# Down projection: sums of activations made with the convolution and kept in HBM, 26 groups by seven instead of 22

## The chip, the cores and the metric

The kernel runs on one core of one Trainium2 chip. A core has a matrix engine (TensorE, PE in the profile), VectorE (DVE), ScalarE (ACT), GpSimd (POOL) and SyncE (SP); each runs its own queue of instructions in order, and they wait for each other by semaphores. The metric is the device time of one execution in microseconds (us), as the median of the runs.

## The reference

One layer of a hybrid block on 256 tokens of width 2048, all in float32: three attentions, a gated merge, and a feed-forward part. Only the last part matters here:

```python
    h2 = rms_norm(x, g_ffn[l])
    u = causal_depthwise_conv(h2 @ w_up[l], conv_w[l], conv_b[l])   # width 3 along the tokens
    u_gate, u_val = jnp.split(u, 2, axis=-1)                        # 5632 columns each
    x = x + (jax.nn.silu(u_gate) * u_val) @ w_down[l]               # w_down: 5632 x 2048
```

## The kernel before

**Precision.** Every float32 operand is split into a hi and a lo part that PE can take: ACT casts (hi), DVE subtracts (lo = value − hi). A product is then three matmuls, hi·hi, lo·hi and hi·lo (`three`, L1308 to L1311); for the weights this splitting is `parts` (L1300 to L1306).

**Up projection** (`u` tiles, L1219 and L1221). For 11 blocks of four column tiles, first gate then value, 16 row tiles of `w_up` in pieces of two. After a block, `conv` (L1131) makes the convolution, and for the value half (`s == 1`) the product with the silu of the gate, `g`; it splits `g` into `aT`, the activations of the down projection with hi and lo beside each other. `later` and `tick` spread these steps over the pieces of the next block. Beside this run `weight_sums` (L1168), one group of the down projection's weights at a time: they load two row tiles of `w_down` into r0 and r1, add, and store the sums T0 and T1 to HBM (`made`).

**Down projection** (`d` tiles). The 44 row tiles of `w_down` are taken in 22 groups of two (`k0`, `k1`), and the 2048 columns in two halves (`nb` = 0 and 1; `n0` = 0 and 1024), so a group is a 2 × 2 by 2 × 2 product of blocks: two tiles of activations by two halves of the tokens, two weight tiles by two blocks of 512 columns. A group *by eight* (`eight`, letter e) makes the eight block products, 24 matmuls in two steps. A group *by seven* (`seven`, letter s) makes seven products of sums of blocks, 21 matmuls in four steps: it needs four sums of activations (FS1 to FS4, made in `forms`) and four of weights: T4|T2 (one tile of 1024 columns) and T1|T3 (another). `gather` puts the products together at the end of a half.

**Sums of activations.** `forms(p)` takes `aT` back together from hi and lo with five operations on DVE, then ACT casts and DVE subtracts the split sums into `sf` (three of them) and into a free place of `aT` (FS4).

**Sums of weights.** T4|T2 comes from HBM in all groups. T1|T3 comes from HBM in the groups of `ALL_FOUR` (twelve); the other ten load the whole of `k0` and make it with two additions (L1371, L1372).

**Order.** `PLANS` gives the order of e and s in each half. Each step has a `prep` (loads, casts, subtractions, additions) and a `use` (matmuls); `prep` runs two steps ahead of `use` in the program (`AHEAD`), and the order on ACT, DVE and SP is kept as written (`keep`). hi and lo tiles have four buffers each (`SBUFS`), so the cast of a step waits until PE has ended with the step four before. Raw weights come into four buffers `raw`, and from the eleventh load on every third into two buffers `more`. Small tiles tagged `junk` have two buffers.

## Time and profile before

| | |
|---|---|
| median of 3 runs | 1472.62 us (1472.32 to 1474.24) |
| span of the profiled execution, first to last instruction | 1469.9 us |
| median less this span | 2.7 us |
| busy: PE, PEld, DVE, ACT, POOL | 1462.8, 1233.4, 1205.1, 895.3, 68.8 us |
| up projection on PE, 2816 matmuls | 747 to 1241 us |
| down projection on PE, first and second half | 1241 to 1357, 1357 to 1466 us |
| DMA traffic | 388.81 MB, mean 265 GB/s |

How it is read: times in the trace run from the first instruction. PE's matmuls overlap, so a busy PE says that it never ran dry, not that it was at its peak; PEld is the loading of weights into PE. A row of the timeline gives start, duration, engine, line, operation and tiles; a bracket at its end the idle time before it and what ended it.

### The profile page before, as it was taken

What the parts mean: (1) busy time and instruction counts of PE and PEld (TensorE: products, weight loads), DVE (VectorE), ACT (ScalarE), POOL (GpSimd) and SP (SyncE); (2) the same over time, 40 slices, a digit from 0 to 9 for tenths busy, and PEclk for the clock granted to TensorE, in tenths of its full rate; (3) what the DMA queues carried; (4) which work ended last, traced back from release to release, by engine and by line L of the source; (5) the groups of instructions that cost most, each with busy time, mean ns of one, the idle gap of its engine ahead of it and who ended that gap; (6) DMA issues with size and microseconds to landing.
All of it is one profiled execution on the core that took longest, in us unless ns stands there. A gap on an engine that the chain in (4) does not pass through costs nothing.

```text
span 1469.9 us, 20741 instructions
## 1 busy us (share of the span) xinstructions
PE 1462.8 (100%) x7327; PEld 1233.4 (84%) x7327; DVE 1205.1 (82%) x1617; ACT 895.3 (61%) x1287; POOL 68.8 (5%) x139
## 2 busy tenths in 40 slices
PE   9999999999999999999999999999999999999998
PEld 7888888888878888888888888888888888888887
DVE  5798767766997799888877888788887886998998
ACT  6755454454664466545657667567676777665774
POOL 1000001021000000000000000000000010000000
PEclk9999999999999999999999999999999999999999
DMA  8697898787766576866776888889888895778995
GB/s 295 202 341 260 265 313 270 226 294 267 256 221 204 204 271 247 287 222 237 273 239 218 302 272 276 294 277 310 295 265 273 280 305 190 249 256 286 334 315 191
DMA packets 163463, 388.81 MB, mean 265 GB/s; under 512 B 14016, under 2 KB 22512, under 8 KB 163360
## 3 DMA queue, kind: packets, MB, share of 16 engines
q1 hardware_dynamic: 150960, 345.34, 70.6%
q0 software_dynamic: 11648, 41.10, 7.3%
q8 instruction: 57, 0.93, 0.3%
q10 hardware_dynamic: 752, 1.06, 0.2%
q14 instruction: 46, 0.38, 0.1%
HBM read 349.70 MB, written 37.75 MB: 264 GB/s over the span
## 4 chain that ended last, share of the span: by engine, by line
PE 94%; DVE 3%; DMA 2%; issue 1%; ACT 0%; SPq 0%; DVEq 0%; ACTq 0%
PE u L1219 21%; PE u L1221 10%; PE d L1310 5%; PE d L1309 5%; PE d L1311 5%; PE g_x L769 4%; PE g_x L770 4%; PE g_x L771 4%; PE s L186 2%; PE s L188 2%; PE f L187 2%; PE f L188 2%; PE f L186 2%; PE s L187 2%; PE b L186 2%; PE b L188 2%
## 5 line engine op out<-in xcount | busy, mean ns | idle before, releaser
L1219 PE MATMUL u<-hT,hi_u 128*128 128x512 f32 x1408 | 442.6, 396 | 0.0
L1221 PEld LDWEIGHTS u<-hT,lo_u 128*128 128x128 f32 x1408 | 264.4, 188 | 63.5 <-DVE lo_u L176 1.1
L1221 PE MATMUL u<-hT,lo_u 128*128 128x256 f32 x1408 | 277.0, 278 | 0.7 <-DVE lo_u L176 0.7
L176 DVE TENSOR_TENSOR lo_u<-raw_u,hi_u 128x1024 fp32r<-128x1024 f32 x176 | 213.2, 1220 | 59.8 <-ACT hi_u L175 59.0
L175 ACT CAST hi_u<-raw_u 128x1024 fp32r<-128x1024 f32 x176 | 183.0, 1049 | 107.0 <-PE u L1219 54.6
L1219 PEld LDWEIGHTS u<-hT,hi_u 128*128 128x128 f32 x1408 | 214.5, 189 | 0.1
L764 ACT CAST hi_g<-raw_g 128x1024 fp32r<-128x1024 f32 (+1 forms) x96 | 91.1, 964 | 53.5 <-PE g_x L770 33.4
L765 DVE TENSOR_TENSOR lo_g<-raw_g,hi_g 128x1024 fp32r<-128x1024 f32 (+1 forms) x96 | 105.0, 1116 | 20.9 <-ACT hi_g L764 20.8
L769 PE MATMUL g_x<-hi_g,xT 128*128 128x512 f32 x251 | 98.8, 394 | 0.0
L770 PE MATMUL g_x<-hi_g,xT 128*128 128x512 f32 x251 | 97.7, 389 | 0.0
L771 PE MATMUL g_x<-lo_g,xT 128*128 128x512 f32 x251 | 96.3, 390 | 0.0
L1148 DVE TENSOR_TENSOR y<-y,z 128x512 f32<-128x512 f32 x88 | 60.7, 691 | 24.4 <-ACT z L1147 20.5
L1147 ACT ACTIVATE z<-u,taps 128x256 f32<-128x256 f32 x176 | 74.7, 496 | 0.0
L1309 PE MATMUL d<-hi_d,aT 128*128 128x512 f32 x176 | 68.5, 389 | 0.0
L1310 PE MATMUL d<-hi_d,aT 128*128 128x512 f32 x176 | 68.5, 389 | 0.0
L1311 PE MATMUL d<-lo_d,aT 128*128 128x512 f32 x176 | 68.1, 389 | 0.0
L175 ACT CAST hi_f<-raw_f 128x1024 fp32r<-128x1024 f32 (+1 forms) x40 | 38.6, 968 | 46.6 <-PE f L187 41.9
L186 PE MATMUL s<-hi_s,xT 128*128 128x512 f32 (+1 forms) x160 | 61.9, 387 | 0.0
L175 ACT CAST hi_b<-raw_b 128x1024 fp32r<-128x1024 f32 x32 | 33.6, 1052 | 45.2 <-PE b L187 23.5
L175 ACT CAST hi_s<-raw_s 128x1024 fp32r<-128x1024 f32 (+1 forms) x40 | 38.3, 959 | 36.8 <-PE s L187 29.3
L186 PE MATMUL f<-hi_f,xT 128*128 128x512 f32 (+1 forms) x160 | 60.4, 377 | 0.0
L188 PE MATMUL s<-lo_s,xT 128*128 128x512 f32 (+1 forms) x160 | 59.1, 369 | 0.0
(498 smaller groups left out, 3265.0 us busy)
## 6 DMA issues: line engine op xcount, KB each, us to landing
raw_u<-in_w_up_dram SPq DMA_DIRECT2D x176, 512.0 KB, 5.4
raw_g<-in_w_in_dram SPq DMA_DIRECT2D x86, 512.0 KB, 5.4
T<-r POOLq DMA_DIRECT2D x64, 512.0 KB, 6.1
r<-in_w_down_dram SPq DMA_DIRECT2D x88, 256.0 KB, 5.2
raw_d<-in_w_down_dram SPq DMA_DIRECT2D x44, 512.0 KB, 5.4
raw_f<-in_w_in_dram SPq DMA_DIRECT2D x32, 512.0 KB, 5.5
raw_s<-in_w_in_dram SPq DMA_DIRECT2D x32, 512.0 KB, 5.4
raw_s<-in_w_down_dram SPq DMA_DIRECT2D x32, 512.0 KB, 5.3
```

What stands on the lines that cost most here:

```text
L175: pin(nc.scalar.copy(hi[:, :m], raw[:, :m]))
L176: pin(nc.vector.tensor_tensor(lo[:, :m], raw[:, :m], hi[:, :m].bitcast(F32), ALU.subtract))
L186: nc.tensor.matmul(o, lhsT=xh, rhs=wh, start=first, stop=False)
L188: nc.tensor.matmul(o, lhsT=xh, rhs=wl, start=False, stop=last)
L769: nc.tensor.matmul(o, lhsT=a[0], rhs=w[0], start=first, stop=False)
L770: nc.tensor.matmul(o, lhsT=a[1], rhs=w[0], start=False, stop=False)
L771: nc.tensor.matmul(o, lhsT=a[0], rhs=w[1], start=False, stop=last)
L1219: nc.tensor.matmul(ps, lhsT=hi[:, j, c], rhs=hT[:, k + j, :], start=first, stop=False)
L1221: nc.tensor.matmul(ps[:, :S], lhsT=lo[:, j, c], rhs=hT[:, k + j, :S], start=False, stop=last)
L1309: nc.tensor.matmul(o, lhsT=ah, rhs=w[0], start=first, stop=False)
L1310: nc.tensor.matmul(o, lhsT=al, rhs=w[0], start=False, stop=False)
L1311: nc.tensor.matmul(o, lhsT=ah, rhs=w[1], start=False, stop=last)
```

## The change

- `unsplit_forms` makes the sums of activations of 16 groups inside `conv`, from `g` before it is split: three operations on DVE into the tile `y`, then a POOL DMA of 256 KB to HBM (`rforms`).
- `forms` no longer computes. It loads one set by a POOL DMA into a `junk` tile, and three ticks later ACT casts and DVE subtracts as before. In the first half ten of these are asked for in steps 1 to 10, in the second half six, one behind each of the first six groups by seven.
- `PLANS` has ten and sixteen groups by seven (8 and 14 before). The first group by seven comes after three by eight instead of five.
- `OWN` (eleven groups) load the two weight tiles whole and make all four weight sums with four additions in place, in `p1`. The other fifteen load both T tiles from HBM; `weight_sums` makes four sums for each of these fifteen, and is started every 9 pieces instead of 7.
- Every second raw load goes to `more`, which has four buffers; the tiles `t13` and `fr` of the down projection's pool go.

```diff
--- before.py
+++ after.py
@@ -35,8 +35,8 @@
 SBUFS = 4
 BLOCKS = 14
 WINDOW = 2
-PLANS = ("eeeee" + "se" * 5 + "sse" + "s" + "eee", "e" + "sse" * 4 + "ssse" + "sssee")
-ALL_FOUR = {(0, 6), (0, 7)} | {(1, p) for p in range(14) if p not in (4, 6, 8, 11)}
+PLANS = ("eee" + "sse" * 5 + "e" + "eee", "e" + "sssse" * 3 + "ssss" + "ee")
+OWN = {(0, p) for p in (1, 2, 4, 5, 7, 8, 9)} | {(1, 1), (1, 5), (1, 9), (1, 13)}
 AHEAD = 2
 GATE_PLANS = (("e" * 8, "essessee", "essessee"), ("eeesssee", "essessee", "essessee"))
 GATE_SEVENS = 4
@@ -48,6 +48,7 @@
 OUT_PLANS = ("eeesssee", "eessseee")
 OUT_SEVENS = 3
 NSEVEN = tuple(plan.count("s") for plan in PLANS)
+NFORM = max(NSEVEN)
 
 
 @with_exitstack
@@ -1162,10 +1163,26 @@
                 yield
             nc.vector.tensor_tensor(a[:, :, S:], g, a[:, :, :S].bitcast(F32), ALU.subtract)
             ended.append(f)
+            if f // 2 < NFORM:
+                yield 1
+                unsplit_forms(f // 2, g, y)
+
+    FS3, FS1, FS2, FS4 = range(4)
+    rforms = {}
+
+    def unsplit_forms(p, g, y):
+        v = g.rearrange("p k (t q) -> p (k t) q", t=NT)
+        r = y.rearrange("p k (t q) -> p (k t) q", t=NT)
+        tt = nc.vector.tensor_tensor
+        tt(r[:, :2], v[:, 0:4:3], v[:, 1:2].to_broadcast([P, 2, P]), ALU.subtract)
+        nc.vector.scalar_tensor_tensor(r[:, FS2], r[:, FS1], -1.0, v[:, 0], ALU.mult, ALU.subtract)
+        tt(r[:, FS4], r[:, FS2], v[:, 2], ALU.add)
+        rforms[p] = dram.tile([P, 512], F32, name=f"rform{p}")
+        nc.gpsimd.dma_start(rforms[p], y.rearrange("p k s -> p (k s)"))
 
     ended = []
     made = {}
-    asked = [(0, p) for p in range(NSEVEN[0])] + [(1, p) for p in range(NSEVEN[1])]
+    asked = [(nb, p) for nb in range(2) for p in range(NSEVEN[nb]) if (nb, p) not in OWN]
 
     def weight_sums(nb, p):
         n0 = nb * PIECE
@@ -1179,16 +1196,13 @@
             yield 1
         yield 1
         add = lambda o, i: tc.keep_in_program_order(nc.vector.tensor_tensor(o, o, i, ALU.add))
-        four = (nb, p) in ALL_FOUR
         add(r[0][:, 0], r[0][:, 1])
-        if four:
-            add(r[0][:, 1], r[1][:, 1])
+        add(r[0][:, 1], r[1][:, 1])
         yield 1
         add(r[1][:, 1], r[0][:, 0])
         add(r[1][:, 0], r[1][:, 1])
-        made[nb, p] = [dram.tile([P, PIECE], F32, name=f"T{j}_{nb}_{p}") for j in range(1 + four)]
-        if four:
-            nc.gpsimd.dma_start(made[nb, p][1], r[0].rearrange("p b n -> p (b n)"))
+        made[nb, p] = [dram.tile([P, PIECE], F32, name=f"T{j}_{nb}_{p}") for j in range(2)]
+        nc.gpsimd.dma_start(made[nb, p][1], r[0].rearrange("p b n -> p (b n)"))
         yield 1
         nc.gpsimd.dma_start(made[nb, p][0], r[1].rearrange("p b n -> p (b n)"))
 
@@ -1220,7 +1234,7 @@
                         else:
                             nc.tensor.matmul(ps[:, :S], lhsT=lo[:, j, c], rhs=hT[:, k + j, :S], start=False, stop=last)
                 n_ticks[0] += 1
-                if asked and n_ticks[0] > 8 and n_ticks[0] % 7 == 2:
+                if asked and n_ticks[0] > 8 and n_ticks[0] % 9 == 2:
                     adding.append([weight_sums(*asked.pop(0)), 0])
                 add_on()
                 tick()
@@ -1244,7 +1258,6 @@
 
     keep = tc.keep_in_program_order
     ov = out[0].rearrange("(t p) d -> p t d", p=P)
-    FS3, FS1, FS2, FS4 = range(4)
     sf = xt_pool.tile([P, 10, 3, 2, P], F32R, tag="xt", name="sf")
 
     def pieces_at(p):
@@ -1256,40 +1269,27 @@
     def form_of(p, f):
         if f == FS4:
             return pieces_of(p)[:, 0, :, 1]
-        if p < 10:
-            return sf[:, p, f]
-        return pieces_at(31 - p).rearrange("p k (f l q) -> p (k f) l q", f=2, l=2)[:, f]
+        return sf[:, p % 10, f]
 
     def forms(p):
 
-        flat = aT[:, 2 * p : 2 * p + 3].rearrange("p k s -> p (k s)").bitcast(F32)
-        v = flat[:, :1024].rearrange("p (k l t q) -> p k l t q", k=2, l=2, t=NT)
-        d = sm.tile([P, 512], F32, tag="junk", bufs=2, name=f"fd_{p}").rearrange("p (f l q) -> p f l q", f=2, l=2)
-        r = down_pool().tile([P, 512], F32, tag="fr", bufs=1, name=f"fr_{p}").rearrange("p (f q) -> p f q", f=4)
-        g = rbc.rearrange("p (k q) -> p k q", k=2)
-        two = flat[:, : 2 * 640].rearrange("p (a b) -> p a b", b=640)[:, :, :512]
-        two = two.rearrange("p a (l t q) -> p a l t q", l=2, t=NT)[:, :, :, 0]
-        tt = nc.vector.tensor_tensor
-        keep(tt(d, two, v[:, 0, :, 1].unsqueeze(1).to_broadcast([P, 2, 2, P]), ALU.subtract))
-        keep(tt(g, v[:, :, 0, 0], v[:, :, 1, 0], ALU.add))
-        keep(tt(r[:, :2], d[:, :, 0], d[:, :, 1], ALU.add))
-        keep(nc.vector.scalar_tensor_tensor(r[:, FS2], r[:, FS1], -1.0, g[:, 0], ALU.mult, ALU.subtract))
-        keep(tt(r[:, FS4], r[:, FS2], g[:, 1], ALU.add))
-        yield
-        to = sf[:, p] if p < 10 else form_of(p, slice(0, 3))
-        last = form_of(p, FS4)
+        r = sm.tile([P, 512], F32, tag="junk", bufs=2, name=f"fr_{p}").rearrange("p (f q) -> p f q", f=4)
+        keep(nc.gpsimd.dma_start(r.rearrange("p f q -> p (f q)"), rforms[p]))
+        yield 3
+        to, last = form_of(p, slice(0, 3)), form_of(p, FS4)
         keep(nc.scalar.copy(to[:, :, 0], r[:, :3]))
         keep(nc.scalar.copy(last[:, 0], r[:, FS4]))
         yield
-        keep(tt(to[:, :, 1], r[:, :3], to[:, :, 0].bitcast(F32), ALU.subtract))
-        keep(tt(last[:, 1], r[:, FS4], last[:, 0].bitcast(F32), ALU.subtract))
+        keep(nc.vector.tensor_tensor(to[:, :, 1], r[:, :3], to[:, :, 0].bitcast(F32), ALU.subtract))
+        keep(nc.vector.tensor_tensor(last[:, 1], r[:, FS4], last[:, 0].bitcast(F32), ALU.subtract))
+        issued.add(f"forms{p}")
 
     turn = [0]
 
     def buffer(name):
         turn[0] += 1
-        if turn[0] > 10 and turn[0] % 3 == 0:
-            return down_pool().tile([P, PIECE], F32, tag="more", bufs=2, name=name)
+        if turn[0] > 10 and turn[0] % 2 == 0:
+            return down_pool().tile([P, PIECE], F32, tag="more", bufs=4, name=name)
         return wp.tile([P, PIECE], F32, tag="raw", name=name)
 
     def load(src, name):
@@ -1351,34 +1351,37 @@
         k0, k1 = 2 * p, 2 * p + 1
         name = f"{n0}_{p}"
         w, raw = {}, {}
-        four = (n0 // PIECE, p) in ALL_FOUR
+        own = (n0 // PIECE, p) in OWN
+        add = lambda o, i: keep(nc.vector.tensor_tensor(o, o, i, ALU.add))
 
         def p0():
-            n = 512 if four else PIECE
+            n = PIECE if own else 512
             raw[0] = load(dv[:, k0, n0 : n0 + n], f"s{n0}_{k0}")
             (w["00"],) = parts(raw[0][:, :512], f"s{n0}_{k0}")
 
         def p1():
             raw[1] = load(dv[:, k1, n0 : n0 + PIECE], f"s{n0}_{k1}")
             w["10"], w["11"] = parts(raw[1], f"s{n0}_{k1}")
+            if own:
+                add(raw[0][:, :512], raw[0][:, 512:])
+                add(raw[0][:, 512:], raw[1][:, 512:])
+                add(raw[1][:, 512:], raw[0][:, :512])
+                add(raw[1][:, :512], raw[1][:, 512:])
 
         def p2():
-            raw[2] = load(made[n0 // PIECE, p][0], f"t{name}")
-            raw[3] = down_pool().tile([P, PIECE], F32, tag="t13", bufs=2, name=f"t13_{name}")
-            if four:
-                keep(nc.sync.dma_start(raw[3], made[n0 // PIECE, p][1]))
-            else:
-                keep(nc.vector.tensor_tensor(raw[3][:, :512], raw[0][:, :512], raw[0][:, 512:], ALU.add))
-                keep(nc.vector.tensor_tensor(raw[3][:, 512:], raw[0][:, 512:], raw[1][:, 512:], ALU.add))
-            w["T4"], w["T2"] = parts(raw[2], f"t42_{name}")
+            if not own:
+                raw[1] = load(made[n0 // PIECE, p][0], f"t{name}")
+                raw[0] = load(made[n0 // PIECE, p][1], f"t13_{name}")
+            w["T4"], w["T2"] = parts(raw[1], f"t42_{name}")
 
         def p3():
-            w["T1"], w["T3"] = parts(raw[3], f"t13_{name}")
+            w["T1"], w["T3"] = parts(raw[0], f"t13_{name}")
 
         def u0():
             three(Y()[0], *a_of(k0, 0), w["00"], first, last)
 
         def u1():
+            assert f"forms{p}" in issued
             three(X()[0][0], *a_of(k1, 0), w["10"])
             three(X()[0][1], *f_of(p, FS4), w["11"])
 
@@ -1444,7 +1447,6 @@
                     keep(nc.vector.tensor_tensor(xr, xr, banks[nb][0][t][n][:, oc], ALU.add))
                     (nc.scalar if nb else nc.gpsimd).dma_start(ov[:, t, xc], xr)
 
-    formed = 0
     after_step = {}
 
     def at(n, do):
@@ -1458,9 +1460,13 @@
         n_done = 0
         if nb == 0:
             at(-1, lambda: start(0))
+            for p in range(10):
+                at(p + 1, lambda p=p: later(forms(p)))
         for i, c in enumerate(plan):
             if c == "s":
                 seven(s, n0, X, Y, s == 0, s == ns - 1)
+                if nb and s + 10 < NFORM:
+                    at(len(steps), lambda p=s + 10: later(forms(p)))
                 s += 1
                 if s == ns:
                     at(len(steps) - 1, lambda nb=nb: later(gather(nb, banks[nb][1])))
@@ -1469,10 +1475,7 @@
                 n_done += 1
                 if n_done == 4:
                     at(len(steps) - 1, lambda nb=nb: residual(nb))
-                if formed < ns and n_done >= 4 - 3 * nb:
-                    at(len(steps) - 2, lambda p=formed: later(forms(p)))
-                    formed += 1
-        assert s == ns and not straight and formed >= ns
+        assert s == ns and not straight
         at(len(steps) - 1, finish)
         at(len(steps) - 1, lambda nb=nb: results(nb))
         if nb == 0:
```

Three places in the order of instructions. First ScalarE in the first half, from the second group by seven (group 1) to the group by eight behind it. Names: `hi_t42_0_1` is the cast of T4|T2 of group 1, `hi_s0_3` is row tile 3 (k1 of group 1), `fr_4` the loaded sums of group 4, `hi_d0_26` row tile 26 of a group by eight. Before:

```order
L1304 CAST hi_s0_3_12155<-raw_s0_3_12153 128x1024
L1281 CAST sf_11814<-fr_2_12147 128x3x128
L1282 CAST aT_6836<-fr_2_12147 128x128
L1304 CAST hi_t42_0_1_12178<-raw_t0_1_12173 128x1024
L1304 CAST hi_t13_0_1_12187<-t13_0_1_12175 128x1024
L1304 CAST hi_d0_28_12199<-raw_d0_28_12197 128x1024
```

And now:

```order
L1304 CAST hi_s0_3_12047<-raw_s0_3_12045 128x1024
L1304 CAST hi_t42_0_1_12061<-raw_s0_3_12045 128x1024
L1280 CAST sf_11826<-fr_2_12008 128x3x128
L1281 CAST aT_6836<-fr_2_12008 128x128
L1280 CAST sf_11826<-fr_3_12010 128x3x128
L1281 CAST aT_6836<-fr_3_12010 128x128
L1304 CAST hi_t13_0_1_12072<-raw_s0_2_12026 128x1024
L1280 CAST sf_11826<-fr_4_12024 128x3x128
L1281 CAST aT_6836<-fr_4_12024 128x128
L1304 CAST hi_d0_26_12090<-raw_d0_26_12088 128x1024
```

Before, one set of sums, which DVE had made, was copied ahead of the casts of T4|T2 and T1|T3. Now sets 2 and 3 are copied between these two casts, and set 4 ahead of the cast for the next group by eight.

Second, VectorE at the same group. Before:

```order
L1305 TENSOR_TENSOR lo_s0_3_12156<-raw_s0_3_12153,hi_s0_3_12155 128x1024
L1371 TENSOR_TENSOR t13_0_1_12175<-raw_s0_2_12128 128x512
L1372 TENSOR_TENSOR t13_0_1_12175<-raw_s0_2_12128,raw_s0_3_12153 128x512
L1305 TENSOR_TENSOR lo_t42_0_1_12179<-raw_t0_1_12173,hi_t42_0_1_12178 128x1024
L1284 TENSOR_TENSOR sf_11814<-fr_2_12147,sf_11814 128x3x128
```

And now:

```order
L1305 TENSOR_TENSOR lo_s0_3_12048<-raw_s0_3_12045,hi_s0_3_12047 128x1024
L1355 TENSOR_TENSOR raw_s0_2_12026<-raw_s0_2_12026 128x512
L1355 TENSOR_TENSOR raw_s0_2_12026<-raw_s0_2_12026,raw_s0_3_12045 128x512
L1355 TENSOR_TENSOR raw_s0_3_12045<-raw_s0_3_12045,raw_s0_2_12026 128x512
L1355 TENSOR_TENSOR raw_s0_3_12045<-raw_s0_3_12045 128x512
L1305 TENSOR_TENSOR lo_t42_0_1_12062<-raw_s0_3_12045,hi_t42_0_1_12061 128x1024
L1305 TENSOR_TENSOR lo_t13_0_1_12073<-raw_s0_2_12026,hi_t13_0_1_12072 128x1024
L1283 TENSOR_TENSOR sf_11826<-fr_2_12008,sf_11826 128x3x128
```

Before, T4|T2 came from HBM as `raw_t0_1`; now it is the result of the four additions, in the buffers of the raw weights, and the tile that ACT casts is the one that DVE has just written.

Third, GpSimd's queue in the first half of the down projection as it is now (before, only the four `xr` loads stood there).

```order
L1277 DMA fr_0_11901<-rform0_7417 128x512
L1277 DMA fr_1_11929<-rform1_7422 128x512
L1404 DMA xr_0_0_0_12166<-xkeep0_6082 128x512
L1404 DMA xr_0_0_1_12168<-xkeep1_6083 128x512
L1404 DMA xr_0_1_0_12170<-xkeep0_6082 128x512
L1277 DMA fr_2_12008<-rform2_7878 128x512
L1404 DMA xr_0_1_1_12172<-xkeep1_6083 128x512
L1277 DMA fr_3_12010<-rform3_7883 128x512
L1277 DMA fr_4_12024<-rform4_8333 128x512
```

The loads of the sums stand in this queue, between those of the residual.

## Prediction

> **What bounds the kernel now.** I began with the page's busy shares by slice and its chain, then asked who waits for whom on TensorE (PE), then for tables by stage, and last for the timelines of one pair of steps in the down projection.
>
> ```profile
> PE   9999999999999999999999999999999999999998
> DVE  5798767766997799888877888788887886998998
> ...
> PE 94%; DVE 3%; DMA 2%; issue 1%; ACT 0%; SPq 0%; DVEq 0%; ACTq 0%
> ```
>
> ```profile
> PE u L1221 <- DVE lo_u L176: 0.7, 1, 0.7
> ...
> PE g_y L769 <- ACT hi_g_0t L764: 0.2, 1, 0.2
> ```
>
> ```profile
> 1270.00:1300.00 30.00, 30.00 (x134) 24.84 (x133) 29.70 (x46) 18.73 (x25) 0.00 (x0) 1.00 0.71 247
> 1300.00:1330.00 30.00, 30.00 (x134) 24.85 (x133) 29.36 (x40) 20.20 (x24) 0.00 (x0) 1.00 0.84 286
> ...
> 1355.00:1385.00 30.00, 30.00 (x134) 24.84 (x133) 27.78 (x40) 20.28 (x25) 3.24 (x6) 1.00 0.97 352
> ```
>
> PE never stops, and its waits (the second block: total, times, longest) come to about 1 us. So the time is the number of matmuls times their spacing. But in the down projection VectorE (DVE, the third busy time in a row of the table) is busy 29.70 of 30 us. It holds PE's pace with nothing to spare, and any chain that runs through it is at the edge.
>
> ```profile
> 1268.28 0.39 PE L1309 MATMUL d<-hi_s,aT 128*128 128x512 f32 x1
> ...
> 1273.04 0.39 PE L1309 MATMUL d<-hi_d,aT 128*128 128x512 f32 x1
> ...
> 1278.47 0.39 PE L1309 MATMUL d<-hi_s,aT 128*128 128x512 f32 x1
> ```
>
> A group by seven is 21 matmuls in 1273.04 − 1268.28 = 4.76 us, one by eight 24 in 5.43. One matmul costs 0.227 us; its 0.39 overlaps the next.
>
> ```profile
> 1280.72 2.35 DVE L1305 TENSOR_TENSOR lo_d<-raw_d,hi_d 128x1024 fp32r<-128x1024 f32 x2
> 1282.99 0.68 DVE L1305 TENSOR_TENSOR lo_s<-raw_s,hi_s 128x512 fp32r<-128x512 f32 x1
> 1283.59 0.68 DVE L1273 TENSOR_TENSOR fd<-aT 128x512 f32<-128x512 f32 x1
> ...
> 1285.52 1.22 DVE L1305 TENSOR_TENSOR lo_s<-raw_s,hi_s 128x1024 fp32r<-128x1024 f32 x1
> 1286.65 0.68 DVE L1371 TENSOR_TENSOR t<-raw_s 128x512 f32<-128x512 f32 x1
> ...
> 1287.86 1.22 DVE L1305 TENSOR_TENSOR lo_t<-raw_t,hi_t 128x1024 fp32r<-128x1024 f32 x1
> 1288.99 0.55 DVE L1284 TENSOR_TENSOR sf<-fr,sf 128x384 fp32r<-128x384 f32 x1
> ...
> 1289.77 1.23 DVE L1305 TENSOR_TENSOR lo_t<-t,hi_t 128x1024 fp32r<-128x1024 f32 x1
> 1290.92 2.35 DVE L1305 TENSOR_TENSOR lo_d<-raw_d,hi_d 128x1024 fp32r<-128x1024 f32 x2
> ```
>
> Start to start, DVE pays 1.13 us for a subtraction of 1024 columns, 0.60 for one of 512, 1.93 for the five operations that make sums of activations (1283.59 to 1285.52), 0.78 for splitting them (1288.99 to 1289.77). A whole seven and eight take it 10.20 us; PE takes 4.76 + 5.43 = 10.19.
>
> **The change, part by part.**
>
> *Matmuls.* 26 groups by seven for 22 save 4 × 3 × 0.227 = **2.7 us**. That is all the change can win on PE.
>
> *The up projection.* 18 of 78 weight additions go, 16 sets of three operations come.
>
> ```profile
> L176 DVE TENSOR_TENSOR lo_u<-raw_u,hi_u 128x1024 fp32r<-128x1024 f32 x176 | 213.2, 1220 | 59.8 <-ACT hi_u L175 59.0
> ```
>
> At the spacings above the additions are 18 × 0.6 = 11 us less, the new sets about 16 × 1 = 16 us more. DVE idles 59.8 us before this one line, which covers the 5 us. I take 0; without the cover an addition held up at the wrong place costs what the one wait above did, 0.7 us, so the ends are +2 (three such) and −0.7 (that wait gone).
>
> *Own weight sums.* In eleven sevens the cast of T4|T2 on ScalarE (ACT) must follow four additions, each on the one before. The spacing of such additions, and a hand-over from ACT to DVE:
>
> ```profile
> 1349.69 0.68 DVE L1417 TENSOR_TENSOR xr<-xr,e 128x512 f32<-128x512 f32 x1
> 1350.41 0.69 DVE L1418 TENSOR_TENSOR e<-e,d 128x512 f32<-128x512 f32 x1
> ```
>
> ```profile
> 1268.29 1.05 ACT L1304 CAST hi_t<-t 128x1024 fp32r<-128x1024 f32 x1 [1.67 <-PE d L1310]
> ...
> 1285.31 0.51 ACT L1281 CAST sf<-fr 128x384 fp32r<-128x384 f32 x1 [1.04 <-DVE fr L1276]
> 1285.72 0.29 ACT L1282 CAST aT<-fr 128x128 fp32r<-128x128 f32 x1
> 1285.97 1.06 ACT L1304 CAST hi_t<-raw_t 128x1024 fp32r<-128x1024 f32 x1
> ```
>
> ```profile
> 1269.37 1.23 DVE L1305 TENSOR_TENSOR lo_t<-t,hi_t 128x1024 fp32r<-128x1024 f32 x1 [0.82 <-ACT hi_t L1304]
> ```
>
> Additions: 3 × 0.72 + 0.69 = 2.85 us. Hand-over: 1269.37 − (1268.29 + 1.05) = 0.03 us. The first ACT row also shows the ring at work: a cast waits for PE to leave the buffer of four steps before.
>
> Take an own seven right behind another seven. Its k1 cast gets its buffer when PE ends the last product with the hi half of the previous k1. From there: cast 1.05, subtraction 1.13, additions 2.85, cast 1.05, four hand-overs 0.12: 6.20 us. PE reaches the first T4|T2 product 23 spacings after that last one began, 5.21 − 0.39 = 4.82 us after it ended. Wait: **1.4 us**. Five sevens stand so (group 7 of the first half; 1, 5, 9, 13 of the second): 7.0 us.
>
> Groups 5 and 9 of the first half follow another own one. From cast to cast DVE and ACT then do 1.13 + 1.13 + 0.60 + 1.13 + 2.85 + 1.05 + 0.1 = 8.0 us, PE 4.76; the wait is at most 3.2, less what the first had in hand. I take 2.8 each, 5.6 us (ends 1.4 and 3.2 each).
>
> Group 1 pays the 1.4 and more: the first seven comes four steps of an eight earlier (4 × 2.7 = 10.9 us), just as DVE ends the convolution's tail, so there is little lead, and its k1 load is one of a burst. I take 4.5 (ends 1.4 and 6). Groups 4 and 8 follow an eight and cost about nothing; group 2 also does, but starts without lead: 1.0.
>
> *Reloading the sums of activations.* Each set now comes by a POOL DMA into one of two buffers, so load p + 2 waits until DVE has subtracted set p. ACT copies a set in its own order, ahead of casts that PE needs next. The nearest load of this size and queue:
>
> ```profile
> xr<-xkeep POOLq DMA_DIRECT2D x8, 256.0 KB, 5.0
> ```
>
> ```profile
> DMA to landing us min/median/max: 3.7/5.0/7.3
> ```
>
> Set 4: after DVE's last subtraction for group 1 come sets 2 and 3, and load 4 can go 0.67 us later; 5.0 to land, 0.66 for two copies (spacings 0.41 and 0.25), 1.05 for the cast of the next eight, 0.1 for hand-overs: 7.5 us. PE has four matmuls left in that time, 0.9 us, so it waits 6.5, then 0.8 for the subtraction: **7.3 us**. Set 8 stands the same way before group 3, with a cast of 512 columns (0.62): 6.1, and then set 9's copies hold the next casts, about 1.5: 7.6. Sets 2, 3 and 6, 7 stand between the casts of T4|T2 and T1|T3 in groups 1 and 2: 1.3 + 1.05 against six matmuls, then the subtraction, 1.7 us each: 3.4. Sum 18.3. With loads of 3.7 it is 15.7, of 7.3 it is 22.9, for two round trips; the nearest row to all is the median, which I take. The page "DMA: Bandwidth & Descriptors" of the Trainium skill (section "Anatomy of one DMA — SWDGE (gpsimd) path") puts such a DMA at about 2.0 us plus its bytes over 436 GB/s, 2.6 us here (an estimate), which would make the time 4.8 us shorter. All eight loads in the row above took longer, so I don't use it.
>
> In the second half sets 10 to 15 are asked for a group or more ahead and stand behind casts that wait for PE anyway. The bytes there, per four sevens and an eight (24.5 us), are 3 × 1.84 MB (256 + 3 × 512 KB with sums from HBM) and 2 × 1.05 (2 × 512 KB): 311 GB/s, and the table above shows 352 carried without a wait. I cost both at nothing; if that cover goes, one late 512 KB load costs about 1.5 us, and I keep +3 for it.
>
> *Sum:* −2.7 + 7.0 + 5.6 + 4.5 + 1.0 + 18.3 = **+33.7**, and I add 1.5 for the second own group of the second half, whose set copies stand beside its additions, and for short waits: **+35 us**. On the execution's span of 1469.9 that is 1505; the median of the runs, 1472.6, has 2.7 us around the span, so I predict **1508 us**.
>
> A check without any DMA: in the first half's five pairs of sevens and an eight DVE needs 10 × 4.0 + 7 × (2.85 + 1.1 for the cast it waits for) + 5 × 2.27 + 10 × 0.78 = 87 us, PE 75. At most a ring of four steps, 4.8 us, is in hand. So 7 us are lost there even if every set is early, 5.6 in the second half by the chain: 1482 at the least by this.
>
> **Rivals.**
>
> 1. *Sets arrive in time* (ACT gets to the copies later than I think). Then only the own sums count: 35 − 18.3 = +17, 1489. For it: POOL has little else to do. Against: the buffer is free only 0.7 us before the copies stand next on ACT. 10%.
>
> 2. *The own sums hide* and only reloads cost: 35 − 18 = +17, 1490. For it, a row of the gate stage, where sums are made the same way:
>
> ```profile
> ACT hi_g_2t L764 <- DVE raw_g L810: 10.9, 4, 2.8
> ```
>
> ACT waited for these additions, PE only the 0.2 us above. Against: there T1|T3 goes first, which needs two additions, not four. 8%.
>
> 3. *All hides*, so no slower: 1469.9, a gain of 0.18%, within the 0.2% that a measurement can tell from none. The place is the ring of four buffers on DVE and ACT. It decides if a cast of T4|T2 comes within 4.82 us of its buffer's release, so if four additions took 1.4 us and not 2.85, and sets landed before they are asked for. DVE's 29.70 of 30 us is against it. 5%.
>
> 4. *The clock falls.*
>
> ```profile
> 1445.00:1470.00 25.00, 20.64 (x92) 16.75 (x90) 19.02 (x23) 9.32 (x10) 0.00 (x0) 0.97 0.40 150
> ```
>
> ```profile
> 1465.41 0.24 PE d L1311
> ```
>
> A mean of 0.97 over 25 us is 1.5 us at half clock, so it halved at about 1468.5, 2.9 us after the last product ended. The two waits of some 6 us are longer than that. How long half clock then lasts no row shows; between nothing and a whole seven (4.76 us) lost each, with loads at their slow end (+4.6): 1508 to 1522, say 1515. 17%. The page "TensorE: Matmul & The Clock Gate" of the Trainium skill (Part 1, "What's actually happening") says half clock comes after an idle window of about 3.4 us and goes after as much sustained work; by that each wait adds 1.7 us (an estimate), 3.4 in all.
>
> **How the numbers follow.** Forecast 60%, its own range 1499 to 1517 (the ends of group 1, the pairs and the loads). With rival 4's to 1526 and rivals 1 and 2 from 1488, a good 8 in 10 are held. Slower: 94%; within 0.2%: 4%; faster: 2% (rival 3 split).
>
> **What would show it.** Right: in the changed profile PE waits for ACT's hi_t by 1 to 3 us in eight or so places, and twice for some 6 us in the 60 us after the first group by seven, with ACT waiting for fr's DMA ahead of them; the second half some 6 to 8 us longer than its matmuls; 12 matmuls fewer; the up projection as long as before. Wrong: ACT's waits for fr short (the sets were early), or PE's waits for hi_t missing behind own sums.

## The result, and the profile after

| | before | after |
|---|---|---|
| median of the runs | 1472.82 us (1472.32 to 1474.24) | 1514.71 us (1512.32 to 1514.87) |
| span of the profiled execution | 1469.9 us | 1510.6 us |
| matmuls of the down projection | 990 | 978 |
| first to last product of the down projection (starts) | 224.2 us | 263.6 us |

The change makes the kernel slower by 2.84% (ratio 1.0284, 95% interval 1.0269 to 1.0299). One of the eleven runs of eights_first_8, below, took 1603.84 us at a granted clock of 0.851; it is counted in that row's median and not in its ratio. The up projection takes 493.3 us in both traces. Of 40.7 us more in the span, 39.4 lie between the first and the last product of the down projection; the other 1.2 are 1.5 us more behind the last product, less 0.2 ahead of the first.

The lines of the page that answer to those of before are TensorE's (PE's) and VectorE's (DVE's) busy tenths, the granted clock in tenths, and the chain that ended last:

```profile
PE   9999999999999999999999999999999996889998
...
DVE  5798676766997899978878888888878766787987
...
PEclk9999999999999999999999999999999998899999
...
PE 87%; DVE 4%; DMA 3%; issue 3%; ACT 3%; POOL 0%; SPq 0%; ACTq 0%; DVEq 0%; POOLq 0%
```

PE's row was nines up to the last digit; now three slices stand at 6 and 8, in the first half of the down projection. PE's share of the chain fell from 94% to 87%; ScalarE (ACT) went from 0% to 3%, issue from 1% to 3%, DMA from 2% to 3%. DVE, which was the engine at its edge, is less busy there than before, so it is not its amount of work that holds PE up. Two rows of the table by stage (PE, PEld, DVE, ACT, POOL; granted clock; DMA) say the same of the worst stretch; before, PE was busy for 30.00 of 30 us in both, and DVE for 29.70 and 29.36:

```profile
1270.00:1300.00 30.00, 18.24 (x57) 11.82 (x57) 15.70 (x24) 11.08 (x20) 3.22 (x6) 0.82 0.50 171
1300.00:1330.00 30.00, 25.85 (x103) 20.05 (x104) 25.36 (x30) 17.90 (x23) 0.00 (x0) 0.90 0.51 163
```

The waits of PE in the down projection (total, times, longest), where before there was none:

```profile
PE d L1309 <- ACT hi_t L1304: 15.3, 10, 2.7
PE d L1309 <- ACT hi_s L1304: 7.5, 2, 6.1
PE d L1309 <- ACT hi_d L1304: 5.7, 1, 5.7
PE d L1311 <- DVE lo_t L1305: 1.1, 2, 0.5
```

There are two main kinds. The ten waits for hi_t, the hi half of a tile of weight sums, are mostly behind own sums. One of them, group 1 of the second half (PE's rows first, then ACT's, then DVE's):

```profile
1400.65 0.61 PE L1311 MATMUL d<-lo_s,aT 128*128 128x512 f32 x2
1402.61 0.50 PE L1309 MATMUL d<-hi_t,sf 128*128 128x512 f32 x1 [1.34 <-ACT hi_t L1304]
...
1396.32 1.05 ACT L1304 CAST hi_s<-raw_s 128x1024 fp32r<-128x1024 f32 x1 [0.47 <-PE d L1310]
1401.51 2.00 ACT L1304 CAST hi_t<-raw_s 128x1024 fp32r<-128x1024 f32 x2 [4.14 <-DVE raw_s L1355]
...
1397.40 1.23 DVE L1305 TENSOR_TENSOR lo_s<-raw_s,hi_s 128x1024 fp32r<-128x1024 f32 x1 [0.21 <-ACT hi_s L1304]
1398.54 0.68 DVE L1355 TENSOR_TENSOR raw_s<-raw_s 128x512 f32<-128x512 f32 x1
1399.26 1.42 DVE L1355 TENSOR_TENSOR raw_s<-raw_s,raw_s 128x512 f32<-128x512 f32 x2
1400.71 0.69 DVE L1355 TENSOR_TENSOR raw_s<-raw_s 128x512 f32<-128x512 f32 x1
```

Cast (1396.32), subtraction (1397.40), four additions (1398.54 to 1401.40), cast (1401.51): one chain, in which ACT and DVE wait for each other in turn, and PE's bracket of 1.34 us is what it is too long by.

The second kind is the two waits of some 6 us. The first, for set 4 of the sums of activations:

```profile
1275.62 1.21 POOL L1277 DMA_DIRECT2D fr<-rform  x2 [11.38 <-DVE aT L1284]
...
1279.97 0.51 ACT L1280 CAST sf<-fr 128x384 fp32r<-128x384 f32 x1 [6.81 <-DMA fr<-rform]
1280.39 0.29 ACT L1281 CAST aT<-fr 128x128 fp32r<-128x128 f32 x1
1280.59 1.04 ACT L1304 CAST hi_d<-raw_d 128x1024 fp32r<-128x1024 f32 x1
...
1281.68 0.79 PE L1309 MATMUL d<-hi_d,aT 128*128 128x512 f32 x1 [5.65 <-ACT hi_d L1304]
```

POOL asks for the set when DVE has split the sets before it (11.38 us of waiting for DVE aT), the load lands 4.35 us later, and behind ACT's wait for it (6.81) stands the cast hi_d that PE needs.

A third kind is small. In group 0 PE loses 1.5 us, and in group 1 another 2.3 ahead of the products with own sums. There ACT waits for weights that are still on their way: T1|T3 of group 0, which comes from HBM, and the two row tiles of group 1.

```profile
1260.20 1.05 ACT L1304 CAST hi_t<-raw_t 128x1024 fp32r<-128x1024 f32 x1 [4.16 <-DMA raw_t<-T]
1262.43 0.62 ACT L1304 CAST hi_s<-raw_s 128x512 fp32r<-128x512 f32 x1 [1.18 <-DMA raw_s<-in_w_down_dram]
1264.76 1.04 ACT L1304 CAST hi_s<-raw_s 128x1024 fp32r<-128x1024 f32 x1 [1.70 <-DMA raw_s<-in_w_down_dram]
```

### The profile page after: what moved, and what is told of

Read it like the earlier page. It is cut to its first block, busy times and chain, and to the rows that moved or that the text cites. A ratio compares the mean times of both kernels' runs of the same rounds, so it can differ in the third digit from the quotient of the medians.

```text
span 1510.6 us, 20765 instructions
## 1 busy us (share of the span) xinstructions
PE 1472.1 (97%) x7315; PEld 1230.2 (81%) x7315; DVE 1206.8 (80%) x1613; ACT 898.0 (59%) x1299; POOL 84.0 (6%) x167
## 2 busy tenths in 40 slices
DMA packets 160840, 384.89 MB, mean 255 GB/s; under 512 B 13952, under 2 KB 22448, under 8 KB 160736
## 3 DMA queue, kind: packets, MB, share of 16 engines
q10 hardware_dynamic: 752, 1.06, 0.2%
## 4 chain that ended last, share of the span: by engine, by line
PE 87%; DVE 4%; DMA 3%; issue 3%; ACT 3%; POOL 0%; SPq 0%; ACTq 0%; DVEq 0%; POOLq 0%
PE u L1233 20%; PE u L1235 10%; PE g_x L770 4%; PE g_x L771 4%; PE g_x L772 4%; PE d L1309 3%; PE d L1310 3%; PE d L1311 3%; PE f L189 2%; PE f L188 2%; PE f L187 2%; PE s L187 2%; PE s L189 2%; PE s L188 2%; PE b L188 2%
## 5 line engine op out<-in xcount | busy, mean ns | idle before, releaser
L1309 PE MATMUL d<-hi_d,aT 128*128 128x512 f32 x144 | 57.1, 396 | 5.7 <-ACT hi_d L1304 5.7
L187 PE MATMUL f<-hi_f,xT 128*128 128x512 f32 (+1 forms) x160 | 60.4, 377 | 0.0
L189 PE MATMUL f<-lo_f,xT 128*128 128x512 f32 (+1 forms) x160 | 59.0, 369 | 0.0
L188 PE MATMUL f<-hi_f,xT 128*128 128x512 f32 (+1 forms) x160 | 59.0, 369 | 0.0
```

Of the source, the lines that this page charges most:

```text
L187: nc.tensor.matmul(o, lhsT=xh, rhs=wh, start=first, stop=False)
L188: nc.tensor.matmul(o, lhsT=xl, rhs=wh, start=False, stop=False)
L189: nc.tensor.matmul(o, lhsT=xh, rhs=wl, start=False, stop=last)
L1309: nc.tensor.matmul(o, lhsT=ah, rhs=w[0], start=first, stop=False)
```

## The experiments

Every run is compared with the kernel before, run beside it on the same chip (its medians were 1471.9 to 1472.7 us). Theory A holds that the loss has three causes: the chain of own sums, the reload of the sets, and TensorE's clock, which falls to half behind the long waits. In the changed kernel 23 matmuls ran at half clock; their spacings (0.43 us or more, less 0.227 each) add up to 1.54 + 1.67 + 2.24 = 5.45 us. So the clock seemed to be the missing part of the prediction.

| run | median us | ratio to before, 95% interval | first to last product, us |
|---|---|---|---|
| changed kernel | 1514.71 | 1.0284 (1.0269 to 1.0299) | 263.6 |
| spread_loads | 1497.84 | 1.0177 (1.0162 to 1.0193) | 248.0 |
| no_own_adds | 1497.10 | 1.0166 (1.0150 to 1.0183) | 245.4 |
| no_adds_spread | 1474.40 | 1.0016 (1.0007 to 1.0026) | 224.7 |
| t13_first | 1501.43 | 1.0197 (1.0182 to 1.0212) | 251.8 |
| behind_eights | 1504.65 | 1.0218 (1.0203 to 1.0234) | 256.2 |
| third_buffer | 1513.84 | 1.0281 (1.0266 to 1.0296) | 264.0 |
| fill_waits | 1516.67 | 1.0304 (1.0286 to 1.0321) | 267.7 |
| fill_again | 1517.47 | 1.0298 (1.0282 to 1.0315) | 268.2 |
| fill_all | 1515.19 | 1.0289 (1.0275 to 1.0303) | 265.4 |
| spread_fill | 1494.06 | 1.0149 (1.0132 to 1.0166) | 246.6 |
| eights_first | 1472.74 | 1.0005 (0.9995 to 1.0015) | 224.0 |
| eights_first_8 | 1470.65 | 0.9985 (0.9976 to 0.9994) | 221.8 |

The last column is of one profiled execution each. Each interval reaches 0.001 to 0.002 to either side, some 2 us, so a difference between two rows is known to about 3 us.

### Taking each cause away, and both

*spread_loads*: the sets of the first half are asked for at the pace at which they are used.

```diff
-            for p in range(10):
-                at(p + 1, lambda p=p: later(forms(p)))
...
+                if not nb:
+                    at(max(s + 1, len(steps) - 6), lambda p=s: later(forms(p)))
                 seven(s, n0, X, Y, s == 0, s == ns - 1)
```

> The changed kernel with one edit: the ten sets of the first half are asked for six steps before their group's first step (one set in some four steps) and no longer one in each step from the second on. Theory A (three causes: the chain of own sums, the reload through two buffers, the clock that falls behind its two long waits): the waits of TensorE for hi_d and hi_s of 5.7 and 6.1 us go, the granted clock stays at 1.0 in the whole down projection, and the waits for hi_t behind a seven stay (2.9, 2.5, 1.5, 2.9 us in the first half, 1.5 us four times in the second). By the gaps of the changed kernel that is 5.8 + 6.3 + about 1.5 behind them, and 5 to 6 us of half clock: 1514.7 - 19, 1492 to 1499. Theory B (the reload alone costs): 1472. Theory C (VectorE has too much to do with the own sums, or the DMA too much to bring, and the reload only shows where that comes up): 1508 to 1515, since the work is the same.

16.9 us under the changed kernel, within theory A's range; B and C fall. The two long waits are gone, and PE's largest now is of another kind:

```profile
PE d L1310 <- DVE aT L1284: 9.5, 4, 2.7
PE d L1309 <- ACT hi_t L1304: 5.4, 4, 1.4
```

In the first half the waits of own sums are seen one product earlier, since the pieces of a set (aT) now queue behind the additions on DVE. One part of the expectation missed: the clock did not stay at 1.0. It fell behind each of three waits of 2.9 us, and 5.9 us of slow spacing are left.

*no_own_adds*: the four additions are left out.

```diff
-            if own:
-                add(raw[0][:, :512], raw[0][:, 512:])
-                add(raw[0][:, 512:], raw[1][:, 512:])
-                add(raw[1][:, 512:], raw[0][:, :512])
-                add(raw[1][:, :512], raw[1][:, 512:])
```

> The changed kernel without the four additions of the eleven groups with own sums (44 additions left out; the raw weights stand in the place of T1 to T4, so the output is not the reference's); loads, casts and subtractions are all there. Theory A: the waits for hi_t behind a seven go (2.9, 2.5, 1.5, 2.9 and four times 1.5 us, and some of the 0.3 to 0.7 us beside them), the waits of 5.7 and 6.1 us for the sets and the half clock behind them stay: 1514.7 - 17, 1494 to 1500. Theory B (reload alone): 1513 to 1515. Theory C (VectorE's work): 44 x 0.7 = 31 us of VectorE go, and with them all waits: 1472 to 1485. If the half clock needs the many waits close together, it goes here too, and the run is some 5 us under that of theory A.

17.6 us under, as theory A has it; the waits of 5.1 and 6.1 us for the sets stay. But at group 1, where the wait of 2.9 us was to go, PE still waits 2.5 us, now for T1|T3. ACT's timeline shows why:

```profile
1265.33 1.04 ACT L1304 CAST hi_t<-raw_s 128x1024 fp32r<-128x1024 f32 x1
1266.28 0.51 ACT L1280 CAST sf<-fr 128x384 fp32r<-128x384 f32 x1
...
1270.14 0.51 ACT L1280 CAST sf<-fr 128x384 fp32r<-128x384 f32 x1 [3.16 <-DMA fr<-rform]
1270.56 0.29 ACT L1281 CAST aT<-fr 128x128 fp32r<-128x128 f32 x1
1270.76 1.04 ACT L1304 CAST hi_t<-raw_s 128x1024 fp32r<-128x1024 f32 x1
```

Without additions ACT is at set 3 earlier, and set 3 has not landed. In the changed kernel it landed while ACT waited for the additions: at this group each cause covers the other.

*no_adds_spread*: both edits.

> Both edits together: the sets asked for six steps ahead, and the 44 own additions left out (the raw weights stand in the place of their sums, so the output is not the reference's). Theory A: nothing is left of the loss, and the 12 matmuls saved are seen: 1472.8 - 2.7, 1468 to 1473, granted clock 1.0 to the end, no wait of TensorE over 0.9 us in the down projection. If something else costs besides (the larger DMA load of the second half, more copies on ScalarE), it shows here: over 1475.

1474.4, a little over the range. PE waits 0.5 us at most. The down projection takes 224.7 us, of which 3.2 us are the short waits for late weights in groups 0 and 1 (in this trace, too, ACT waits 4.47 us for T1|T3 of group 0). So the two causes hold nearly the whole loss. Together the edits win 40.3 us, 5.8 more than their sum of 34.5; by the ratios, which take out the differences between chips, it is 6.3, and the intervals allow some 4 us either way. What this surplus is, is asked further down.

### Inside the two causes

*t13_first*: in own groups the sums that need two additions go first.

```diff
         def p2():
...
-            w["T4"], w["T2"] = parts(raw[1], f"t42_{name}")
+            if own:
+                w["T1"], w["T3"] = parts(raw[0], f"t13_{name}")
+            else:
+                w["T4"], w["T2"] = parts(raw[1], f"t42_{name}")
...
-        steps.extend(((p0, u0), (p1, u1), (p2, u2), (p3, u3)))
+        steps.extend(((p0, u0), (p1, u1), (p2, u3), (p3, u2)) if own else ((p0, u0), (p1, u1), (p2, u2), (p3, u3)))
```

> The changed kernel with one edit: in the eleven groups with own sums the cast of T1 and T3, which needs the first two of the four additions, stands ahead of that of T4 and T2, which needs all four; TensorE's order is turned likewise. Additions, loads and bytes are the same. Theory A1 (the latency of the chain cast, four additions, cast, subtraction sets the waits behind a seven): the chain gets two additions shorter, 2 x 0.72 = 1.4 us; the four waits of 1.5 us in the second half go, and each of 2.9, 2.5, 1.5, 2.9 us in the first gets some 1.4 us shorter: 6 + 5.6 and with the first half clock 1.5: 1514.7 - 12, 1500 to 1505; the waits of some 6 us for the sets stay. Theory A2 (VectorE has too much work in these groups, whatever its order): 1512 to 1516.

13.3 us for the same 44 additions in another order: theory A1. The cast of the first sums now begins while DVE still adds (ACT, then DVE, second half of the columns):

```profile
1392.99 1.05 ACT L1304 CAST hi_t<-raw_s 128x1024 fp32r<-128x1024 f32 x1 [2.70 <-DVE raw_s L1355]
...
1392.18 1.42 DVE L1355 TENSOR_TENSOR raw_s<-raw_s,raw_s 128x512 f32<-128x512 f32 x2
1393.64 0.69 DVE L1355 TENSOR_TENSOR raw_s<-raw_s 128x512 f32<-128x512 f32 x1
```

ACT waited 2.70 us here and 4.14 in the changed kernel, the 1.44 of two additions. So the length of the chain sets the wait, not DVE's load.

*behind_eights*: own sums only behind groups by eight.

```diff
-OWN = {(0, p) for p in (1, 2, 4, 5, 7, 8, 9)} | {(1, 1), (1, 5), (1, 9), (1, 13)}
+OWN = {(0, p) for p in (0, 2, 4, 6, 8)} | {(1, 0), (1, 4), (1, 8), (1, 12)}
```

> The changed kernel with one edit: own sums in the groups that stand directly behind an eight (0, 2, 4, 6, 8 of the first half, 0, 4, 8, 12 of the second: nine groups), all others from HBM; order within a group as in the changed kernel. Theory A: directly behind an eight, TensorE has 24 matmuls and 5.4 us more in the steps in which the chain runs, so the waits of 2.5, 1.5, 2.9 us and four of 1.5 us go or shrink under 1 us; the two of some 6 us for the sets stay: 1514.7 - 11, 1500 to 1506. Rival (any own sum costs its additions wherever it stands): 9 of 11 are left, 1510 to 1513.

10.1 us are won, with 36 additions in place of 44; so the place counts, as the prediction's ring of four buffers has it; in the second half PE's longest wait is 0.5 us. In the first half the sets' waits grew: group 1 now waits 5.9 us for T1|T3, because ACT, no longer held up by additions there, waits for set 3, as in no_own_adds.

*third_buffer*: a third buffer for the sets.

```diff
-        r = sm.tile([P, 512], F32, tag="junk", bufs=2, name=f"fr_{p}").rearrange("p (f q) -> p f q", f=4)
+        pool = (down_pool(), dict(tag="fr", bufs=1)) if p % 3 == 2 else (sm, dict(tag="junk", bufs=2))
+        r = pool[0].tile([P, 512], F32, name=f"fr_{p}", **pool[1]).rearrange("p (f q) -> p f q", f=4)
```

> The changed kernel with one edit: three buffers in place of two for the sets that come back from HBM (every third set goes to one of its own). Theory A1 (the two buffers of the round trip are the cause, as the prediction has it): set 4 can be asked for one set earlier, and the two waits of some 6 us shrink by about the distance of two sets, some 5 us each, and the half clock with them: 1514.7 - 14, 1498 to 1504. Theory A2 (the pace is the cause: one set in each step is asked for, and each holds up ScalarE in order, whatever the buffers): the waits only move to later sets: 1508 to 1515.

1513.84: theory A2. ACT's waits for sets go from 15.6 us to 11.9, and PE's waits for hi_d and hi_s to 2.8 and 5.5 us at most, but PE's total for hi_t grew from 15.3 to 17.4:

```profile
ACT sf L1281 <- DMA fr<-rform: 11.9, 2, 6.5
```

```profile
PE d L1310 <- ACT hi_t L1305: 17.4, 11, 2.7
PE d L1310 <- ACT hi_s L1305: 6.3, 3, 5.5
PE d L1310 <- ACT hi_d L1305: 2.8, 1, 2.8
```

The 0.9 us won lie within the intervals. With a set asked for in every step, a set that is late still stands ahead of a cast that PE needs, only at other places. One buffer more does not help at this pace, and spread_loads, which changes the pace and keeps two buffers, takes the long waits away.

### What the half clock costs

*fill_waits*: matmuls on a tile of zeros keep PE busy in the three waits of groups 1 to 3, so that the clock should stay up while every wait for data stays.

```diff
+    def fill(n, o, w):
+        for _ in range(n):
+            nc.tensor.matmul(o, lhsT=zero[0], rhs=w, start=False, stop=False)
...
+                if n0 == 0 and k == 26:
+                    fill(24, X()[0][0], last_w[0])
...
+            if (n0, p) == (0, 3):
+                fill(26, X()[0][0], last_w[0])
...
+            if (n0, p) == (0, 1):
+                fill(11, X()[0][0], w["10"][0])
```

> The changed kernel with 61 matmuls more, whose stationary tile is all zeros (they add nothing to the sums), put where TensorE waits: 11 ahead of T4 and T2 of the second group of the first half (wait 2.9 us), 24 ahead of the eight behind it (5.8 us), 26 ahead of the fourth group (6.3 us); 0.227 us each, so that they end a little before the operand comes. No wait gets shorter for the data; only TensorE is no longer idle in them. Theory A with the clock as a cause of its own: the granted clock stays at 1.0, and the 23 matmuls that ran at half clock behind the waits (1.54 + 1.67 + 2.24 us) run at full speed: 1514.7 - 5.4, 1507 to 1511. Rival (the clock costs nothing here, since VectorE and ScalarE are behind in those places anyway): 1513 to 1516.

A miss, and inconclusive: 1516.7 us. 2.3 us of the wait for hi_d were left behind the zeros, and half clock came behind it and, by the place of the waits, behind two others further on.

*fill_again*: the zeros move over activations, so that they hold no weight buffer.

```diff
-                    fill(24, X()[0][0], last_w[0])
+                    fill(24, X()[0][0], aT[:, 31])
```

> As the run before with 61 matmuls on a tile of zeros in the three waits (11, 24, 26), but their moving operand is now a block of activations that nothing writes any more, and no longer a weight tile, so that they hold no buffer that ScalarE waits for. What was open: whether the half clock costs time of its own. Theory A (it does): no half clock behind the three waits, the waits themselves unchanged for the data, 1514.7 - 5.4, 1507 to 1511; a half stretch can still follow one of the 2.9 us waits further on, as in other runs (1.6 us more, to 1513). Rival (the stall costs the same at either clock): 1514 to 1517.

1517.5, a miss again, and 13.7 us at half clock. At full clock PE got through group 1 faster, but the set for the next group came no earlier, so 2.4 us of the wait for it were left behind the zeros.

*fill_all*: enough zeros.

```diff
-                    fill(24, X()[0][0], aT[:, 31])
+                    fill(33, X()[0][0], aT[:, 31])
...
-                fill(26, X()[0][0], aT[:, 31])
+                fill(33, X()[0][0], aT[:, 31])
...
-            if (n0, p) == (0, 1):
+            if (n0 // PIECE, p) in ((0, 1), (0, 5), (0, 9), (1, 5)):
```

> As the run before (matmuls on a tile of zeros, on activations that nothing writes any more), but enough of them that TensorE is hardly idle: 11 ahead of T4 and T2 of groups 1, 5 and 9 of the first half, 33 ahead of the eight behind group 1 and 33 ahead of group 3, 8 ahead of T4 and T2 of group 5 of the second half. What was open: the run before still had 13.7 us at half clock, since 2.4, 1.9 and 2.8 us of its waits were left; so it did not take away what it was to take away. Here the granted clock should stay at 1.0. Theory A (every us lost at half clock is lost): 1514.7 - 5.4, 1508 to 1511. Theory A' (what is lost ahead of a wait for a set, 1.54 and 1.67 us, is taken out of that wait, since the set comes when it comes; only the 2.24 us behind the second long wait count): 1511 to 1514. Rival (it costs nothing): 1514 to 1517. About 0.5 us can be added where the zeros overrun a wait.

The clock is full in all the down projection, and the time is 1515.2 us: the changed kernel's own, within the intervals. The table by stage of this run; against the rows of the changed kernel above, the clock is 1.00 where it was 0.82 and 0.90:

```profile
1270.00:1300.00 30.00, 27.19 (x113) 20.11 (x112) 17.55 (x27) 11.14 (x20) 3.23 (x6) 1.00 0.48 162
1300.00:1330.00 30.00, 28.65 (x122) 22.21 (x121) 22.38 (x27) 16.16 (x21) 0.00 (x0) 1.00 0.53 173
```

DVE and ACT together do about what they did in these 60 us. Ahead of group 3 the zeros end too late: the cast of hi_s is done at 1304.80 and the product starts at 1305.40, so about half a us of the time is the zeros' own. By the ratios this run is 0.7 us above the changed kernel, give or take 3. So in this kernel the half clock costs less than these runs can tell (some 2 to 3 us): where PE is slow there, it would else have waited longer for the next set. As a cause of its own, of the 5.4 us that were asked for, theory A's third falls.

*spread_fill*: the same question where no set is waited for, in spread_loads, with 11 zeros ahead of the first form in groups 1, 5 and 9.

```diff
             three(X()[0][0], *a_of(k1, 0), w["10"])
+            if n0 == 0 and p in (1, 5, 9):
+                fill(11, X()[0][0], aT[:, 31])
```

> The run with the sets asked for six steps ahead (1497.8), with 11 matmuls on a tile of zeros in each of its three waits of 2.9 us (groups 1, 5 and 9 of the first half, ahead of the first form), so that no half clock follows them; the data come when they came. What was open: the two edits alone gained 16.9 and 17.6 us, together 40.3, so 5.8 more than their sum, while taking the half clock out of the changed kernel gained nothing. Reading 1 (behind these waits TensorE has no wait for a set that takes up what it lost, so the 5.9 us lost at half clock in this kernel are real, as the like 5.4 us are in the one without additions, and that is the 5.8): 1490.5 to 1493.5. Reading 2 (the half clock costs nothing here either, and the 5.8 are something else): 1496 to 1499.

1494.06 (1493.2 to 1496.4), between the ranges of the two readings and nearer to the first: 3.8 us won of 5.9 (4.1 by the ratios, give or take 3.4, so a gain is clear and its size is not). (The profiled execution, the slowest of four, had one half stretch of 3.4 us left, in the second half.) Clock in the first 20 us, spread_loads and then this run:

```profile
1260.00:1280.00 20.00, 16.04 (x56) 11.77 (x55) 14.25 (x17) 9.40 (x13) 1.19 (x3) 0.83 0.90 330
```

```profile
1260.00:1280.00 20.00, 17.48 (x71) 12.46 (x70) 14.37 (x19) 9.31 (x13) 1.60 (x3) 1.00 0.87 315
```

Here the half clock is paid for. The trace of spread_loads suggests why: behind the first half stretches ACT's next wait is for PE to free a buffer, where in the changed kernel it was for a set:

```profile
1276.34 1.05 ACT L1304 CAST hi_s<-raw_s 128x1024 fp32r<-128x1024 f32 x1 [2.09 <-PE d L1310]
```

So a slow PE makes what is behind it later. This reading would cover the surplus of 5.8: each edit alone leaves slow clock (5.9 and 5.4 us) and the wait of 2.5 to 2.9 us at group 1, which either cause keeps alive, and only both together remove them. What the clock costs was measured in spread_loads alone; for no_own_adds, and so for the split of the surplus, it is argued.

### A version without the loss

*eights_first* has all the remedies: sets six steps ahead, T1|T3 first, own sums behind eights; and five eights in front, so that the first group by seven has more lead.

```diff
-PLANS = ("eee" + "sse" * 5 + "e" + "eee", "e" + "sssse" * 3 + "ssss" + "ee")
+PLANS = ("eeeee" + "sse" * 5 + "ee", "e" + "sssse" * 3 + "ssss" + "ee")
```

> A version that should keep the gain: 26 groups by seven as in the changed kernel, the sets asked for six steps ahead; the own sums only in groups that stand directly behind an eight (0, 2, 4, 6, 8 of the first half, 0, 4, 8, 12 of the second, nine in place of eleven); in these the cast of T1 and T3, which needs two additions, stands before that of T4 and T2, which needs four; and five eights at the front of the first half in place of three. Theory A: no wait is left, 12 matmuls fewer, so 1468 to 1473 (before 1472.8). Theory C (VectorE's or the DMA's amount of work): 36 own additions are still there, and all bytes, so 1490 or more.

1472.7, level with before, with 36 own additions and no fewer bytes: theory C is out. Groups 0 and 1 wait no longer either, with the first group by seven two eights later; no run changes that alone. One wait is left:

```profile
PE d L1310 <- DVE aT L1284: 1.6, 1, 1.6
```

*eights_first_8*: `len(steps) - 8` in place of `- 6`.

> The version with own sums behind eights and five eights in front, its sets asked for eight steps ahead in place of six: the one wait that was left there (1.7 us, TensorE for the pieces of a set whose load took 6.2 us) goes. Theory A: 12 matmuls fewer than before and no wait: 1469 to 1472, ratio to before 0.998 to 1.000. Rival (a set asked for earlier holds up the loads behind it, and the wait comes back elsewhere): 1472 to 1475.

1470.65 us. In its trace PE waits for nothing in the down projection, which takes 221.8 us, 2.4 under before. That is the 12 matmuls, nearly whole: 0.15% (0.06 to 0.24), at the edge of what can be told.

## Why the prediction was right, and where it was off

The main terms of the sum are found in the trace, at the places where the prediction has them. Some of the causes behind them are not those that it gave, and one place was left out.

- *Matmuls.* 978, 12 fewer, and worth the 2.7 us that were given for them: eights_first_8 shows 2.4 of it, once nothing else is lost.
- *Up projection.* Costed at nothing; 493.3 us in both.
- *Own sums behind a plain seven.* Predicted 1.4 us each. PE's bracket is 1.34 in the row above, and the spacing lost is 1.5 to 1.6 in all five. The step was confirmed twice: a chain two additions shorter and a place with more lead both took these waits nearly away. The second groups of a pair (5 and 9), predicted at 2.8 each, lost 2.5 and 2.9.
- *Groups 0, 1 and 2.* 4.5 were predicted for group 1 as own sums. It lost 5.2: 2.9 at the own sums, and 2.3 in two shorter waits ahead of them, which are the late row tiles (the prediction named the burst of loads, without a price of its own). Group 0, for which nothing was set down, lost 1.5 to the late T1|T3. The cause at group 1 was put too simply, too: no_own_adds shows that the late set 3 stands behind the additions there. Group 2 lost 1.06 us, and 1.0 was predicted, but that is luck: PE does not wait at T4|T2, where own sums would show. It waits at T1|T3, whose cast (1292.18) stands behind the copies of sets 6 and 7 (from 1290.95). So the loss belongs with the 1.7 that the prediction gave for those copies. It takes both causes: in no_own_adds and in spread_loads alike group 2 loses nothing.
- *Reload.* Predicted 7.3 and 7.6 for sets 4 and 8 with waits of 6.5 and 6.1; PE's brackets were 5.7 and 6.1. The load of set 4 took 4.35 us to land, against 5.0 taken from the row of other loads; the sixteen loads of sets took these times from issue to landing:

```profile
DMA to landing us min/median/max: 2.8/5.5/8.8
```

  The median bears out the choice of a row of this trace (5.0) over the 2.6 us that the page "DMA: Bandwidth & Descriptors" of the Trainium skill gives in "Anatomy of one DMA — SWDGE (gpsimd) path"; even the shortest is longer. The reason was put wrongly in one point: "one of two buffers" was named as what delays a load. POOL does wait for a buffer (11.38 us in the row above), but a third buffer won only 0.9 us. What counts is that ten sets are asked for in ten steps.
- *The copies of sets between casts*, and what follows the two long waits (0.8 + 1.5 + 3.4 us of the 18.3), were, but for the 1.06 of group 2, not seen as waits of their own. In their place PE ran 23 matmuls at half clock, 5.45 us of spacing. fill_all suggests that it is the same time: with the clock up, PE is idle instead, and the end moves by less than can be told.
- *Rival 4*, the clock, came true as an event and not as a cost. The time of 1515 that it gave is nearly the time measured, but fill_all leaves it no share in it that these runs can tell.
- *The size.* The terms give 35 us, and the span grew by 40.7. PE's spacing above 0.227 us, added up by place, against the terms (the numbered groups are those of the first half):

  | place | predicted, us | lost, us |
  |---|---|---|
  | group 0 | 0 | 1.7 |
  | group 1, with the copies of sets 2 and 3 | 4.5 + 1.7 | 7.5 |
  | group 2, with the copies of sets 6 and 7 | 1.0 + 1.7 | 1.5 |
  | the two long waits and what follows | 7.3 + 7.6 | 16.5 |
  | five own sums behind a plain seven | 7.0 | 8.5 |
  | groups 5 and 9 | 5.6 | 5.9 |
  | short waits elsewhere | 1.5 | 0.5 |

  Apart from group 0, which had no term, no place is off by more than 1.6 us. A little is lost at each wait: the matmul after it comes at 0.34 us and the next few at 0.23 to 0.26, not 0.227. The 1.2 us outside the products had no term either. The rest of the way from 1508 to 1514.7 is that the median lies 4.1 us above the profiled span, the fastest of four executions, and not 2.7.
- *The second half's DMA*, costed at nothing with +3 in reserve, cost nothing: PE's waits there are the four behind own sums, and eights_first_8, which moves more bytes (390.66 MB against 384.89), has none.

## What to carry to other kernels

Removing work from the engine that looks full can lose time if it turns independent operations into a chain through two engines, or puts a load's landing into an in-order queue: count the operations between a buffer's release and the product that needs it, and compare them with what the waiting engine still has to do. Ask for reloaded data at the pace of its use, some steps ahead; one buffer more did not help an order that asks for everything at once. Two causes that cover each other can't be weighed by taking away one at a time; take away both as well.
